# The last 1 MB of a batched 64x64 matmul: two stores of 512 KB by GpSimd in place of four of 256 KB by SyncE and ScalarE

## The chip, the core and the metric

The kernel runs on one core of a Trainium2 chip. The metric is the device time of one execution in microseconds (us). Three runs of the kernel before gave 128.67, 128.90 and 128.98 us, median 128.9 us. The profile comes from an execution of its own, told below.

## What is computed

```python
def reference(a, b):          # a, b: [1024, 64, 64] float32
    return np.matmul(a, b).astype(np.float32)
```

There are 1024 independent products of 64x64 matrices. Inputs are 2 x 16 MB, the output is 16 MB, all in float32.

## The kernel before, in words

**Tiling.** The output is worked off in `n_t` = 16 tiles of 64 matrices (1 MB each, `t` = 0 to 15); inputs are loaded for 128 matrices at a time (`s` = 0 to 7). For each tile, matrices of `a` are transposed (`turn_a`, VectorE), spread into a block-diagonal tile (`spread`, VectorE with some ScalarE), matrices of `b` are cast and turned (`turn`), and `products` (L201) multiplies four matrices at a time on TensorE into PSUM. `evacuate` (L238) copies the products from PSUM into the tile `o_sb`, which holds the whole result tile: 128 partitions x 8 groups (`gh`) x 1 KB. In the last tile (L269 to L273) the 16 steps go through four PSUM tiles of four steps each. ScalarE evacuates the first and third, VectorE the second and fourth, in four copies each (L247). So after ScalarE's first four copies groups 0 and 1 of `o_sb` are ready, after VectorE's first four groups 2 and 3, after ScalarE's last four groups 4 and 5, and after VectorE's last four groups 6 and 7.

**Stores.** `multiply` leaves a list of closures in `held[t]` (L280), which `store(t)` (L193) calls after the tile's work has been written down. Each closure calls `put(lo, n)` (L255), which starts one DMA from `n` groups of `o_sb` to `o_v[t]`. In HBM each partition's group is a run of 1 KB. For tiles 0 to 14, `put` writes four groups (512 KB) and `store_queue` (L80) names GpSimd. For the last tile, `put` writes two groups (256 KB), four times, and the queue comes from `LAST_QUEUE` (L51): SyncE for `lo` = 0, 2 and 6, ScalarE for `lo` = 4.

**Queues.** Nearly all loads, and the stores of tiles 0 to 14, are issued by GpSimd, on one queue that the profile names q0 (software_dynamic). SyncE's DMAs are on q1, ScalarE's on q10 (both hardware_dynamic). All of them are served by the core's 16 DMA engines. The order of the instructions on each engine is the order in the program text (`tc.manual_schedule`, L282). A store by GpSimd takes one of eight completion semaphores in turn and first waits until that semaphore's previous DMA has landed.

**The end.** After the last tile SyncE waits in turn for the semaphores of all DMAs and engines, every engine drains, and two rounds of barriers follow (L353 in the profile).

Of the kernel before, what the change touches and what calls it, by code (L numbers as in the profile page):

```python
# [12 lines left out]
def kernel(  # L13
# [14 lines left out]
    nc = tc.nc  # L28
# [4 lines left out]
    n_t, n_s = B // 64, B // 128  # L33
# [14 lines left out]
    }  # L48
    PAIRS = (1, 2, 3, 4, 5, 6, 7)
    BY_QUARTERS = (0, 1)  # L50
    LAST_QUEUE = {0: nc.sync, 2: nc.sync, 4: nc.scalar, 6: nc.sync}  # L51
    B_QUEUE = {0: nc.sync, 1: nc.scalar}

    a_v = a.rearrange("(s g h) (mp v) k -> s h g mp (v k)", h=4, g=32, v=16)
# [21 lines left out]
    warm = consts.tile([128, 2], fp32)  # L76
    a_tiles, b_tiles, at_tiles, bbf_tiles = {}, {}, {}, {}
    held = {}

    def store_queue(t, lo):  # L80
        return nc.gpsimd if t < n_t - 1 else LAST_QUEUE[lo]

    def load_a(s, hs=range(4)):
        if 0 in hs:
# [116 lines left out]
    def products(t, g0, n, o_ps, us=(0, 1)):  # L201
        bd = bd_tiles[t % N_BD]
        b_bf = bbf_tiles[t // 2][:, 16 * (t % 2) : 16 * (t % 2) + 16]
        split = len(us) == 1
        if t == n_t - 2:
            at_bd = bd[:].rearrange("p g w h mp vo -> p w g (h mp vo)")
            at_bd = at_bd.bitcast(bf16).rearrange("p w g (c u) -> p w g c u", u=2)
            steps = [
                (g, w, u, g % 2)
                for even in range(g0, g0 + n, 2)  # L210
                for w in range(4)
                for u in us
                for g in (even, even + 1)
            ]
        else:
            at_bd = bd[:].rearrange("p g (j wl) h mp vo -> p j g (wl h mp vo)", j=2)
            at_bd = at_bd.bitcast(bf16).rearrange("p j g (c u) -> p j g c u", u=2)
            steps = [(g, j, u, None) for g in range(g0, g0 + n) for j in range(2) for u in us]
        for g, w, u, par in steps:
            gl = (g - g0) // 2  # L220
            if par is None:
                place = o_ps[:, gl, 2 * (g % 2) + w, :]
                first = gl % 2 == 0 and w == 0 and g % 2 == 0
                final = gl % 2 == 1 and w == 1 and g % 2 == 1
            else:
                place = o_ps[64 * par : 64 * par + 64, gl, w, :]
                first = gl % 2 == 0 and w == 0
                final = gl % 2 == 1 and w == 3
            nc.tensor.matmul(  # L229
                place,  # L230
                at_bd[:, w, g, :, u],
                b_bf[:, g, 64 * u : 64 * u + 64],
                start=u == 0 and (first or not split),
                stop=u == 1 and (final or not split),
                skip_group_check=split,
            )

    def evacuate(t, g0, n, o_ps, o_sb, copy):  # L238
        rows = o_sb[:, g0 // 2 : (g0 + n) // 2]
        if t == n_t - 2:  # L240
            copy(rows, o_ps[:])
            return
        rows = rows.rearrange("p gh (j wl) n -> p gh j wl n", j=2)
        o_ps = o_ps[:].rearrange("p gl (par j) n -> p gl par j n", par=2)
        for par in range(2):
            for wl in range(2):
                copy(  # L247
                    rows[64 * par : 64 * par + 64, :, :, wl, :],
                    o_ps[64 * wl : 64 * wl + 64, :, par, :, :],
                )  # L250

    def multiply(t):
        o_sb = o_pool.tile([128, 8, 4, 64], fp32, name="o_sb")

        def put(lo, n):  # L255
            store_queue(t, lo).dma_start(  # L256
                out=o_v[t, :, lo : lo + n, :],
                in_=o_sb[:, lo : lo + n].rearrange("p gh w n -> p (gh w n)"),
            )

        act, dve = nc.scalar.copy, nc.vector.tensor_copy
        if t == n_t - 2:
            halves = [o_psum.tile([128, 4, 4, 64], fp32, name="o_ps") for _ in range(2)]
            for u in range(2):
                for half in range(2):
                    products(t, 8 * half, 8, halves[half], (u,))
                    if u == 1:
                        evacuate(t, 8 * half, 8, halves[half], o_sb, act)
        elif t == n_t - 1:  # L269
            for g0 in range(0, 16, 4):  # L270
                o_ps = t_psum.tile([128, 2, 4, 64], fp32, name="t_ps")
                products(t, g0, 4, o_ps)
                evacuate(t, g0, 4, o_ps, o_sb, dve if g0 % 8 else act)  # L273
        else:
            for g0 in (0, 8):
                o_ps = o_psum.tile([128, 4, 4, 64], fp32, name="o_ps")
                products(t, g0, 8, o_ps)
                evacuate(t, g0, 8, o_ps, o_sb, act)
        n = 2 if t == n_t - 1 else 4
        held[t] = [lambda lo=lo: put(lo, n) for lo in range(0, 8, n)]  # L280

    with tc.manual_schedule():  # L282
        load_first_a()
# [27 lines left out]
        for t in range(n_t):  # L311
            s, half = t // 2, t % 2
            multiply(t)
            if t == 1:
                spread_all(3)
            elif half == 0 and s + 1 < n_s and t:
                turn_a(s + 1, 0)
                turn_a(s + 1, 1)
                spread_all(t + 2)
            elif half and s + 1 < n_s:  # L320
                if s + 1 == n_s - 1:
                    spread_all(t + 2)
                turn(s + 1, 0)
                turn(s + 1, 1)
                if s + 1 < n_s - 1:
                    spread_all(t + 2)
            store(t)
# [30 lines left out]
```

## Time and profile before

| | us |
|---|---|
| median of 3 runs (lowest to highest) | 128.9 (128.67 to 128.98) |
| the profiled execution's own time | 128.72 |
| its span, first to last instruction | 126.9 |
| busy: DVE / ACT / POOL / PE | 104.0 / 93.7 / 64.1 / 53.1 |
| bytes: HBM read / written | 33.55 MB / 16.78 MB |
| share of the 16 DMA engines' span: q0 / q1 / q10 | 87.8% / 6.6% / 4.9% |

The span is shorter than the execution's own time by 1.8 us, which lie before the first and after the last instruction. The profile's rows give, for each line of the kernel, the engine, the operation, its output and input tiles, and busy time with the mean of one. POOL is GpSimd, SP is SyncE, and a "q" behind an engine's name stands for its sequencer, which issues DMAs and waits. Clock times are us from the start of the span. A DMA issue is the instruction that starts a transfer. Its landing is when the last of the 16 DMA engines has reported; each engine reports for itself, and these landing events are in the trace.

### The profile page before, as it was taken

The page shows a single profiled execution, that of the slowest core. Times are in us where ns is not written, and L with a number is a line of the kernel's source. Part 1 is how long each engine was busy: PE and PEld are TensorE (multiplying, and loading weights), DVE is VectorE, ACT ScalarE, POOL GpSimd, SP SyncE. Part 2 cuts the span into 40 slices and gives each one's busy share as a digit, 9 for nine tenths or more (in the row PEclk, how much of TensorE's full clock was granted, in tenths as well). Part 3 has the DMA queues.
Part 4 walks back from the last instruction along what each step waited for, and adds up shares of the span by engine and source line. Part 5 has one row for each costly group of instructions (what it writes and reads, how often), then busy time and mean ns, then how long its engine had stood idle before and what let it go on. Part 6 is the DMA issues. An engine that isn't in the chain of part 4 may idle for free.

```text
span 126.9 us, 2686 instructions
## 1 busy us (share of the span) xinstructions
PE 53.1 (42%) x1088; PEld 50.1 (39%) x1088; DVE 104.0 (82%) x109; ACT 93.7 (74%) x146; POOL 64.1 (50%) x92
## 2 busy tenths in 40 slices
PE   0000005740945057825751677057810863079200
PEld 0000005730935057815750677057800853079100
DVE  4998993499999999999999997995949789780900
ACT  2258019999396969997999799959897299999700
POOL 8981217973546545545574545475555564333100
PEclk9999999999595555555775555955555579756995
DMA  2999999999999999999999999999999999999993
GB/s 62 379 368 307 305 285 212 219 212 209 288 283 254 275 294 297 285 285 267 271 274 303 297 287 275 263 271 283 305 288 289 270 275 275 383 401 396 345 342 104
DMA packets 10123, 35.81 MB, mean 282 GB/s; under 512 B 1536, under 2 KB 2560, under 8 KB 8448
## 3 DMA queue, kind: packets, MB, share of 16 engines
q0 software_dynamic: 7392, 30.41, 87.8%
q1 hardware_dynamic: 1632, 2.88, 6.6%
q10 hardware_dynamic: 1088, 2.36, 4.9%
q8 instruction: 8, 0.13, 0.4%
q14 instruction: 3, 0.02, 0.0%
HBM read 33.55 MB, written 16.78 MB: 396 GB/s over the span
## 4 chain that ended last, share of the span: by engine, by line
DMA 62%; POOL 9%; ACT 8%; DVE 6%; issue 6%; PE 4%; DVEq 0%; POOLq 0%
DMA b_sb<-in_b_dram 32%; DMA a_sb<-in_a_dram 15%; DMA out_dram<-o_sb 15%; ACT o_sb L247 6%; DVE b_bf L127 4%; PE o_ps L229 3%; POOL at_bd L289 3%; POOL at_bd L302 3%; DVE o_sb L247 2%; POOL a_sb L89 2%; ACT at_bd L173 2%; PE t_ps L229 1%; POOL out_dram L256 1%; POOL b_sb L119 0%; DVEq L353 0%
## 5 line engine op out<-in xcount | busy, mean ns | idle before, releaser
L229 PE MATMUL o_ps<-b_bf,at_bd 128*128 128x64 bf16 (+1 forms) x1024 | 50.8, 230 | 65.0 <-ACT o_sb L247 25.9
L229 PEld LDWEIGHTS <-at_bd 128*128 128x128 bf16 (+1 forms) x1088 | 50.1, 125 | 67.9 <-issue 42.5
L247 ACT COPY o_sb<-o_ps 64x512 f32<-64x512 f32 x112 | 64.9, 580 | 11.2 <-PE o_ps L229 9.7
L256 POOL DMA_DIRECT2D out_dram<-o_sb x30 | 24.4, 814 | 28.3 <-ACT o_sb L247 9.3
L127 DVE STREAM_TRANSPOSE b_bf<-b_sb 128x1024 f32<-128x1024 f32 x14 | 29.8, 2182 | 3.3 <-DMA b_sb<-in_b_dram 3.2
L150 DVE STREAM_TRANSPOSE at_sb<-a_sb 128x1024 f32<-128x1024 f32 x12 | 22.5, 1947 | 2.7 <-issue 1.3
L173 DVE COPY at_bd<-at_sb 32x1024 f32<-32x1024 f32 x34 | 23.8, 700 | 1.0
L92 POOL DMA_DIRECT2D a_sb<-in_a_dram x24 | 14.0, 585 | 18.3 <-DMA a_sb<-in_a_dram 10.5
L119 POOL DMA_DIRECT2D b_sb<-in_b_dram x28 | 15.9, 576 | 6.8 <-DMA out_dram<-o_sb 5.6
L163 DVE COPY at_bd<-at_sb 32x512 f32<-32x512 f32 x30 | 13.1, 438 | 3.8 <-POOL at_bd L302 3.2
L173 ACT COPY at_bd<-at_sb 32x1024 f32<-32x1024 f32 x14 | 14.6, 1043 | 2.0 <-DVE at_sb L150 1.8
L191 ACT CAST b_bf<-b_sb 128x2048 bf16<-128x2048 f32 x2 | 3.7, 1896 | 6.1 <-DMA b_sb<-in_b_dram 6.1
L247 DVE COPY o_sb<-t_ps 64x256 f32<-64x256 f32 x8 | 3.4, 422 | 3.5 <-PE t_ps L229 3.4
L135 ACT CAST a_bf<-o_sb 128x1024 bf16<-128x1024 f32 x3 | 3.0, 1044 | 4.0 <-DMA o_sb<-in_a_dram 4.0
L140 DVE STREAM_TRANSPOSE at_sb<-a_bf 128x512 f32<-128x512 f32 x4 | 4.1, 1050 | 0.4 <-ACT a_bf L135 0.3
L140 DVE STREAM_TRANSPOSE at_sb<-a_sb 128x512 f32<-128x512 f32 x4 | 3.9, 1034 | 0.4 <-DMA a_sb<-in_a_dram 0.4
L288 DVE MEMSET at_bd<- 128x4096 f32 x1 | 3.5, 3472 | 0.8 <-issue 0.8
L289 POOL MEMSET at_bd<- 128x4096 f32 x1 | 3.5, 3511 | 0.3 <-POOLq L342 0.3
L302 POOL MEMSET at_bd<- 128x4096 f32 x1 | 3.5, 3530 | 0.0
L285 ACT ACT_TABLE_LOAD x1 | 1.3, 1283 | 2.3 <-issue 2.3
L247 ACT COPY o_sb<-t_ps 64x256 f32<-64x256 f32 x8 | 2.9, 367 | 0.1
L89 POOL DMA_DIRECT2D a_sb<-in_a_dram x4 | 2.7, 692 | 0.0
(11 smaller groups left out, 7.2 us busy)
## 6 DMA issues: line engine op xcount, KB each, us to landing
out_dram<-o_sb POOLq DMA_DIRECT2D x30, 512.0 KB, 9.4
a_sb<-in_a_dram POOLq DMA_DIRECT2D x28, 256.0 KB, 9.6
b_sb<-in_b_dram POOLq DMA_DIRECT2D x28, 256.0 KB, 9.6
o_sb<-in_a_dram ACTq DMA_DIRECT2D x2, 512.0 KB, 6.8
o_sb<-in_a_dram SPq DMA_DIRECT2D x2, 512.0 KB, 5.8
out_dram<-o_sb SPq DMA_DIRECT2D x3, 256.0 KB, 5.2
out_dram<-o_sb ACTq DMA_DIRECT2D x1, 256.0 KB, 5.1
b_sb<-in_b_dram SPq DMA_DIRECT2D x1, 0.5 KB, 15.9
```

The costliest lines, as they stand in the source:

```text
L92: nc.gpsimd.dma_start(out=rows, in_=ap_v[s, h])
L119: nc.gpsimd.dma_start(out=pair[32 * h : 32 * h + 32, 0], in_=bp_v[s, h])
L127: nc.vector.transpose(cols[:, u], rows[:, u])
L140: nc.vector.transpose(at_tiles[s][:, h].rearrange("p g w mp vo -> p w vo g mp"), rows.bitcast(fp32).rearrange("p (vo w kp) -> p w vo kp", ...
L150: nc.vector.transpose(cols[:, 2 * h : 2 * h + 2].rearrange("p mp vo w g -> p (mp vo) w g"), rows[:, 2 * h : 2 * h + 2].rearrange("p mp vo ...
L163: copy(bd[rows, 8 * i : 8 * i + 8, :, h, :, :].rearrange("p g w mp vo -> p (g w) (mp vo)"), at_sb[block : block + 32, h].rearrange("p g w ...
L173: copy(bd[rows, :, :, h, :, :].rearrange("p g w mp vo -> p (g w) (mp vo)"), at_sb[rows, half].rearrange("p g w mp vo -> p (g w) (mp vo)"),)
L229: nc.tensor.matmul(place, at_bd[:, w, g, :, u], b_bf[:, g, 64 * u : 64 * u + 64], start=u == 0 and (first or not split), stop=u == 1 and ( ...
L247: copy(rows[64 * par : 64 * par + 64, :, :, wl, :], o_ps[64 * wl : 64 * wl + 64, :, par, :, :],)
L256: store_queue(t, lo).dma_start(out=o_v[t, :, lo : lo + n, :], in_=o_sb[:, lo : lo + n].rearrange("p gh w n -> p (gh w n)"),)
L289: nc.gpsimd.memset(bd_tiles[1][:], 0.0)
L302: nc.gpsimd.memset(bd_tiles[2][:], 0.0)
```

## The change

The last tile is stored as all the others are: by GpSimd, in two DMAs of four groups (512 KB). The two quarters of a half that were separate DMAs are now one, so it waits for both ScalarE's and VectorE's copies of that half. `LAST_QUEUE` and `store_queue` go.

```diff
-    LAST_QUEUE = {0: nc.sync, 2: nc.sync, 4: nc.scalar, 6: nc.sync}
...
-    def store_queue(t, lo):
-        return nc.gpsimd if t < n_t - 1 else LAST_QUEUE[lo]
...
         def put(lo, n):
-            store_queue(t, lo).dma_start(
+            nc.gpsimd.dma_start(
                 out=o_v[t, :, lo : lo + n, :],
                 in_=o_sb[:, lo : lo + n].rearrange("p gh w n -> p (gh w n)"),
             )
...
-        n = 2 if t == n_t - 1 else 4
-        held[t] = [lambda lo=lo: put(lo, n) for lo in range(0, 8, n)]
+        held[t] = [lambda lo=lo: put(lo, 4) for lo in (0, 4)]
```

## The prediction

> **What bounds the kernel now.** The change touches only the last tile's stores, so I read the end of the kernel and leave the rest. First the time by stage (sums of PE, PEld, DVE, ACT and POOL, then the granted clock, the busy share of the DMA engines and GB/s):
>
> ```profile
> 113.00:115.00 2.00, 1.92 (x73) 1.79 (x70) 0.83 (x1) 1.81 (x3) 0.73 (x1) 0.50 1.01 397
> 115.00:117.00 2.00, 2.00 (x62) 1.94 (x58) 0.00 (x0) 2.00 (x3) 0.72 (x1) 0.62 1.03 393
> 117.00:119.00 2.00, 1.11 (x39) 0.99 (x34) 1.72 (x5) 1.93 (x6) 0.79 (x2) 1.00 1.02 352
> 119.00:121.00 2.00, 0.00 (x0) 0.00 (x0) 1.66 (x4) 0.80 (x3) 0.00 (x0) 1.00 0.97 345
> 121.00:123.00 2.00, 0.00 (x0) 0.00 (x0) 0.00 (x0) 0.00 (x0) 0.00 (x0) 1.00 1.01 341
> 123.00:125.00 2.00, 0.00 (x0) 0.00 (x0) 0.00 (x0) 0.00 (x0) 0.00 (x0) 0.59 0.87 294
> ```
>
> From 121 on no engine computes any more, and the DMA engines are still full: the end is set by the backlog of stores. The second thing to see is the last column. The same full engines move 393 to 397 GB/s up to 117 and 341 to 352 GB/s after it, although until 119.8 only GpSimd's queue has data packets. So the pace of a store at the very end is not the pace of a store before.
>
> Second, the timeline of the end (start, length):
>
> ```profile
> 114.98 1.93 ACT L241 COPY o_sb<-o_ps 128x1024 f32<-128x1024 f32 x2 [0.16 <-PE o_ps L229]
> ...
> 116.79 3.03 ACT L247 COPY o_sb<-t_ps 64x256 f32<-64x256 f32 x8
> 117.20 0.75 POOL L256 DMA_DIRECT2D out_dram<-o_sb  x1 [0.16 <-issue]
> 117.22 3.49 DVE L247 COPY o_sb<-t_ps 64x256 f32<-64x256 f32 x8 [3.39 <-PE t_ps L229]
> 118.32 2.81 SPq L256 DMA_DIRECT2D out_dram<-o_sb  x3
> 119.85 0.40 ACTq L256 DMA_DIRECT2D out_dram<-o_sb  x1
> ```
>
> The data of the last tile are complete at 117.22 + 3.49 = 120.71, and the last quarter is issued at 120.73 (SyncE's third). Third, the time from issue to landing, over all stores:
>
> ```profile
> out_dram<-o_sb POOLq DMA_DIRECT2D x30, 512.0 KB, 9.4
> ...
> out_dram<-o_sb SPq DMA_DIRECT2D x3, 256.0 KB, 5.2
> out_dram<-o_sb ACTq DMA_DIRECT2D x1, 256.0 KB, 5.1
> ```
>
> The landing events give the order. GpSimd's last eight stores have their last engine's report at 113.24, 114.54, 115.85, 117.13, 118.42, 119.74, 121.35 and 123.34. The steps are 1.30, 1.31, 1.28, 1.29, 1.32, then 1.61 and 1.99. The four quarters land at 123.54, 124.25, 124.98 and 125.66. The last one opens the close: SyncE goes through its remaining waits at 0.06 us each, is drained at 126.18, and two rounds of barriers end at 126.9, which is 1.24 us behind the last landing. Fourth, GpSimd has a drain of its own in the close:
>
> ```profile
> L353 POOLq DRAIN  x1: 6697/6697/6697, 117.2 to 117.2; - x1
> ```
>
> It ends at 117.18 + 6.70 = 123.88, which is 0.53 us behind the last landing of GpSimd's own queue (123.34). Now it ends 2.3 us ahead of SyncE and costs nothing.
>
> **The change part by part.**
>
> *Removed: four issues and their waits.* SyncE's three (0.40, 0.84 and 0.41 us) and ScalarE's one (0.40 us) lie behind no compute of theirs and beside a full DMA backlog. ScalarE has no work after 119.82. Worth nothing by themselves. Their transfers go too: 1024 packets of 1 KB at a mean of 48.2 ns, over 16 engines 3.08 us.
>
> *Added: two issues by GpSimd.* GpSimd issues 0.29 us after its producer ends (ScalarE's L241 pair ends at 116.91, the issue starts at 117.20), where SyncE needs 0.03 us, and an issue takes it 0.75 us. The first half waits for VectorE's fourth copy, 118.94: issue at 119.23 to 119.98. The second waits for VectorE's eighth, 120.70: issue at 120.99 to 121.74. Nothing is queued on GpSimd behind them but its drain. The semaphores whose turn it is were last used by the stores that landed at 113.24 and 114.54, so no wait for a semaphore is added. The first quarter was issued at 118.32 and could move from then on; now nothing of the last tile moves before 119.23. That 0.9 us is covered while GpSimd's queue is not empty: alone, its packets in flight at 119.78 are still 1.87 us of work for each engine, so they end near 121.65 on average.
>
> Is the cover enough? A GpSimd store in a short queue is the one issued at 116.28: its first engine reported 3.58 us after the issue, the last 5.06 us after. By this the first half is down between 122.81 and 124.29, the second between 124.57 and 126.05. The 5.06 holds some waiting behind the store ahead, so this is no firm floor, but it leaves little to spare: if the cover is gone, the second half lands up to 126.05.
>
> The Trainium skill (DMA: Bandwidth & Descriptors, section "Latency and other measured facts") gives about 0.6 us to the first byte for a DMA of SyncE or ScalarE and about 1 us for one of GpSimd, which speaks against the change: by it the two halves would cost 0.4 us where the queue is empty and nothing where it is not. No run here shows a first byte with an empty queue.
>
> *Moved: 1 MB from q1 and q10 to q0.* The two halves are 256 packets of 4 KB. Their duration is what I can't read off for sure. By the packets of 113 to 115 it is 165 ns; in 120 to 122 it is 187 ns. For the engine that is last, the step from one store's last landing to the next shows the same: 1.30 us in the steady part, 1.61 us for the store of 116.28, when only one or two stores stood ahead of it and no other queue moved much. The third, 1.99, shared its engines with the quarters, so it is left out. From 121.35, when the store of 116.28 is down, three stores remain (that of 117.20, now alone, and the two halves):
>
> - at 1.30 each: 121.35 + 3.90 = 125.25, against 125.66 before: 0.41 us earlier;
> - at 1.61 each: 121.35 + 4.83 = 126.18: 0.52 us later.
>
> I take 1.61. At the end never more than two stores wait, as with the row that gave 1.61; the 1.30 comes from rows with four and more in flight. Both ends are kept for the range.
>
> *The close.* SyncE's waits behind the last landing are about as many as now (two HWDGE semaphores fewer in the list, GpSimd's ones nearer to its start): 0 to 0.1 us. What is late next is GpSimd's drain. Now it must outlast the last landing of the kernel: if it ends 0.53 us behind it, as before, that is 126.18 + 0.53 = 126.71, and SyncE is through at 126.18 + 0.52 = 126.70. They tie: nothing added.
>
> **Sum.** +0.52 on the end, 0 in the close: span 126.9 + 0.5 = 127.4, and 128.72 + 0.52 = 129.24 for the profiled execution. The median of the runs is 0.18 above the profiled execution's time, so the forecast for the runs is 128.9 + 0.5 = **129.4 us**.
>
> **The rivals.** A measurement of this kernel can tell about 0.3% (0.39 us) from no change; so "same" is 128.5 to 129.3.
>
> 1. *GpSimd's queue keeps its steady pace* (faster). The 4 KB packets take 165 ns, the two halves need 2 x 8 x 0.165 = 2.64 us on each engine where the quarters need 3.08 us: 0.44 less by packets, 0.41 less by the steps: 128.5 us. For it: 165 ns stays the 25th percentile of GpSimd's packets right to 121. Against it: the rate fell to 345 GB/s with that queue alone. It decides if the step is at or under 1.30.
>
> 2. *Bytes are bytes* (same). From 117 on the engines move 341 to 352 GB/s whether the packets are GpSimd's or the quarters'. If that rate is the limit, 1 MB takes as long through either queue and the end stays: a step near 1.45 gives 121.35 + 4.35 = 125.70, +0.04 us: 128.9 us. For it: the flat last column. Against it: the slowest engine, not the mean, ends the kernel, and on GpSimd's queue its report came up to 1.1 us behind the mean one (store of 117.20), on the last quarter 0.6 us behind. The Trainium skill (same page, section "Issuing engines are not separate DMA queues") states this rival: the DMAs of all issuers run on the same 16 engines, and another issuer saves only issue time. By it the sum would be zero.
>
> 3. *The drain becomes the bound* (slower still). If GpSimd's drain is not tied to the landing but takes a fixed time after its last issue (123.88 - 117.95 = 5.92 us), it now ends at 121.74 + 5.92 = 127.66. The barrier that began at 126.20 then begins at 127.68: +1.48 us, 130.4 us. For it: one profile can't tell the two apart. Against it: an end 0.53 us behind the last landing looks like a wait for the transfers.
>
> **How the numbers follow.** Forecast (+0.5, slow step) 0.42; rival 1 0.20; rival 2 0.28; rival 3 0.10. Slower is the forecast and rival 3, 0.52; same 0.28; faster 0.20. The range goes from rival 1 (128.5) to rival 3 (130.4); the forecast with its neighbours alone would be 129.0 to 129.8.
>
> **What would show it.** GpSimd's last two issues at 119.2 and 121.0, each 0.75 us. The steps between the last landings of GpSimd's last three stores: 1.6 means the forecast, 1.45 rival 2, 1.3 rival 1. The rate in 121 to 125. The end of GpSimd's drain: 0.5 us behind the last landing is the forecast's, and near 127.7 with landings by 126.2 is rival 3. I am wrong if a first packet of the second half comes after the queue ran dry for long (a gap in the DMA share near 122.5 to 123.5), or if the stores of tile 14 themselves land at other times.

## The result and the profile after

The changed kernel takes 128.94 us (median of 14 runs, 128.76 to 129.11), the kernel before, beside it, 128.73 us (14 runs, 128.55 to 129.02). The ratio is 1.0016 with a 95% interval of 1.0009 to 1.0024: **0.21 us slower** (0.12 to 0.31). The interval leaves no doubt that it is slower, but the loss is less than half of the forecast 0.5 us, and 128.94 lies inside what the prediction called "same". The profiled execution of the changed kernel has its own time of 128.95 us and a span of 127.2 us.

The timeline of the end, in the changed kernel (start, length; lines are four or five lower than before):

```profile
116.67 3.02 ACT L243 COPY o_sb<-t_ps 64x256 f32<-64x256 f32 x8
117.07 0.75 POOL L252 DMA_DIRECT2D out_dram<-o_sb  x1 [0.16 <-issue]
117.17 3.48 DVE L243 COPY o_sb<-t_ps 64x256 f32<-64x256 f32 x8 [3.47 <-PE t_ps L225]
119.44 0.75 POOL L252 DMA_DIRECT2D out_dram<-o_sb  x1 [1.61 <-DVE o_sb L243]
121.20 0.75 POOL L252 DMA_DIRECT2D out_dram<-o_sb  x1 [1.01 <-issue]
```

What starts between 116 and 117.2 does so 0.05 to 0.13 us earlier than before. GpSimd's two new issues come at 119.44 and 121.20, each 0.55 us behind VectorE's copy (118.89 and 120.65). The stages of the end, with the columns as before:

```profile
113.00:115.00 2.00, 1.92 (x72) 1.78 (x70) 0.70 (x1) 1.81 (x3) 0.60 (x1) 0.50 1.02 399
115.00:117.00 2.00, 2.00 (x59) 1.94 (x56) 0.00 (x0) 2.00 (x3) 0.75 (x1) 0.61 1.02 385
117.00:119.00 2.00, 1.06 (x37) 0.94 (x33) 1.76 (x5) 1.92 (x7) 0.75 (x1) 1.00 1.00 348
119.00:121.00 2.00, 0.00 (x0) 0.00 (x0) 1.61 (x4) 0.69 (x2) 0.75 (x1) 0.74 1.02 360
121.00:123.00 2.00, 0.00 (x0) 0.00 (x0) 0.00 (x0) 0.00 (x0) 0.75 (x1) 0.50 0.93 315
123.00:125.00 2.00, 0.00 (x0) 0.00 (x0) 0.00 (x0) 0.00 (x0) 0.00 (x0) 0.50 0.83 293
```

The DMA engines are no longer quite full in 121 to 123 (0.93 against 1.01 before), so the queue did run partly dry. Yet the last landing moves little: 125.76 against 125.66. The landing events of GpSimd's last four stores are at 121.24, 122.81, 124.37 and 125.76, steps of 1.57, 1.56 and 1.39 us. The first two of these are the stores of tile 14, which landed at 121.35 and 123.34 before.

The rest of the loss is behind the last landing. These are the close's rows (L353 before, L348 after): count, shortest/median/longest in ns, and the starts of the first and the last. Before, from 125.6 on:

```profile
L353 SPq EVENT_SEMAPHORE  x7: 27/28/28, 125.7 to 126.0; - x7
L353 SPq DRAIN  x2: 7/10/13, 126.1 to 126.2; - x2
L353 POOLq EVENT_SEMAPHORE  x2: 17/17/17, 126.2 to 126.3; - x2
```

After, from 125.7 on:

```profile
L348 SPq EVENT_SEMAPHORE  x7: 28/28/28, 125.8 to 126.1; - x7
L348 SPq DRAIN  x2: 7/10/13, 126.2 to 126.3; - x2
L348 POOLq DRAIN  x1: 5202/5202/5202, 121.2 to 121.2; - x1
L348 POOLq EVENT_SEMAPHORE  x1: 17/17/17, 126.4 to 126.4; - x1
```

SyncE goes through seven waits in both, the first of which is the one for the last landing. It is drained at 126.18 before and at 126.28 after, 0.52 us behind the landing each time. But GpSimd's drain, over at 123.88 before, now ends at 121.18 + 5.20 = 126.38, which is 0.10 us after SyncE, and GpSimd's barrier wait (the last row) follows it. From the last landing to the end of the span it takes 1.40 us; before it took 1.28 (the prediction has 1.24, from a span rounded down to 126.9).

### The profile page after: what moved, and what is told of

Its sections match the earlier page's. It is cut to its first block, busy times and chain, and to the rows that moved or that the text cites. A ratio compares the mean times of both kernels' runs of the same rounds, so it can differ in the third digit from the quotient of the medians.

```text
span 127.2 us, 2684 instructions
## 1 busy us (share of the span) xinstructions
PE 54.3 (43%) x1088; PEld 51.3 (40%) x1088; DVE 103.9 (82%) x109; ACT 93.7 (74%) x146; POOL 64.8 (51%) x94
## 4 chain that ended last, share of the span: by engine, by line
DMA 48%; DVE 20%; POOL 10%; ACT 6%; issue 6%; PE 4%; POOLq 1%; DVEq 1%; ACTq 0%
DMA b_sb<-in_b_dram 26%; DMA a_sb<-in_a_dram 15%; DVE b_bf L123 9%; DMA out_dram<-o_sb 7%; ACT o_sb L243 5%; DVE at_bd L159 5%; DVE at_sb L146 3%; PE o_ps L225 3%; POOL at_bd L284 3%; POOL at_bd L297 3%; POOL a_sb L85 2%; DVE o_sb L243 2%; POOL out_dram L252 2%; PE t_ps L225 1%; DVE at_bd L169 1%
## 5 line engine op out<-in xcount | busy, mean ns | idle before, releaser
L225 PE MATMUL o_ps<-b_bf,at_bd 128*128 128x64 bf16 (+1 forms) x1024 | 52.0, 233 | 63.7 <-ACT o_sb L243 24.8
L225 PEld LDWEIGHTS <-at_bd 128*128 128x128 bf16 (+1 forms) x1088 | 51.3, 127 | 66.7 <-issue 41.9
L252 POOL DMA_DIRECT2D out_dram<-o_sb x32 | 26.4, 824 | 31.2 <-DMA a_sb<-in_a_dram 9.3
L115 POOL DMA_DIRECT2D b_sb<-in_b_dram x28 | 15.1, 547 | 7.6 <-DMA out_dram<-o_sb 5.7
```

What stands on the lines that cost most here:

```text
L115: nc.gpsimd.dma_start(out=pair[32 * h : 32 * h + 32, 0], in_=bp_v[s, h])
L225: nc.tensor.matmul(place, at_bd[:, w, g, :, u], b_bf[:, g, 64 * u : 64 * u + 64], start=u == 0 and (first or not split), stop=u == 1 and ( ...
L252: nc.gpsimd.dma_start(out=o_v[t, :, lo : lo + n, :], in_=o_sb[:, lo : lo + n].rearrange("p gh w n -> p (gh w n)"),)
```

## The experiments

The table has, from each kernel's profile, the last landing, the times at which SyncE and GpSimd are through with their drains, and the time from the last landing to the end of the span ("close"); then the time against the kernel before on the same chip, with its interval.

| | last landing | SyncE | GpSimd | close | against before |
|---|---|---|---|---|---|
| before | 125.66 | 126.18 | 123.88 | 1.28 | |
| changed | 125.76 | 126.28 | 126.38 | 1.40 | +0.16% (+0.09 to +0.24) |
| e1 four quarters, GpSimd | 126.09 | 126.46 | 126.79 | 1.48 | +0.33% (+0.21 to +0.44) |
| e2 two halves, SyncE | 125.65 | 125.80 | 123.38 | 0.92 | **-0.28% (-0.41 to -0.16)** |
| e3 half GpSimd, half SyncE | 125.77 | 125.93 | 125.24 | 0.93 | -0.23% (-0.34 to -0.13) |
| e4 half SyncE, half GpSimd | 125.72 | 126.37 | 126.30 | 1.43 | +0.09% (-0.02 to +0.20) |
| e5 before, 6 spare loads | 125.87 | 126.02 | 123.68 | 0.92 | -0.10% (-0.19 to -0.01) |
| e6 before, 7 spare loads | 126.04 | 126.62 | 123.91 | 1.35 | +0.39% (+0.25 to +0.53) |
| e7 changed, no wait for data | 126.06 | 126.58 | 126.68 | 1.40 | +0.37% (+0.19 to +0.55) |
| e8 changed, long queue | 126.13 | 126.65 | 126.75 | 1.40 | +0.43% (+0.30 to +0.57) |
| e9 e8, idle engines | 126.41 | 126.93 | 127.03 | 1.41 | +0.49% (+0.23 to +0.75) |
| e10 changed, reversed places | 126.01 | 126.53 | 126.63 | 1.40 | +0.08% (-0.07 to +0.23) |

A landing differs by some 0.1 to 0.25 us between profiles of kernels whose stores are alike (changed and e10: 125.76 and 126.01). The close does not: 1.40 or 1.41 in all five kernels with two GpSimd stores at the end. In all twelve profiles, 0.77 to 0.79 us are left from the later of the two drains to the end of the span, so the close is that later drain and a fixed rest.

Landings can be compared more closely with two means over the 16 DMA engines' reports: that of the last store, less that of the store which GpSimd issues near 106 us in every kernel. This is 10.08 to 10.12 us in the four kernels whose last tile goes out by SyncE and ScalarE (before, e2, e5, e6), 10.24 and 10.27 with one half by GpSimd (e3, e4), 10.30 to 10.34 with all of it by GpSimd and issued when its data are ready (changed, e1, e10), and 10.24, 10.21 and 10.11 in e7, e8 and e9, where the stores don't wait for their data.

### e1 to e4: which engine issues what

My theories were a late start of GpSimd's stores (S), the pace of its packets (P) and its drain (D).

```diff
 e1  LAST_QUEUE = {0: nc.gpsimd, 2: nc.gpsimd, 4: nc.gpsimd, 6: nc.gpsimd}
 e2  LAST_QUEUE = {0: nc.sync, 4: nc.sync}      # with n = 4
 e3  LAST_QUEUE = {0: nc.gpsimd, 4: nc.sync}    # with n = 4
 e4  LAST_QUEUE = {0: nc.sync, 4: nc.gpsimd}    # with n = 4
```

(All four are edits of the kernel before.)

> The last tile goes out in four stores of 256 KB, all by GpSimd. Theory S (late start: an issue by GpSimd that waits for two engines starts 0.55 us after the later one and takes 0.75 us, so the queue runs partly dry in 121 to 123, DMA share 0.92): a quarter can start before its half is complete, the first near 118.7 instead of 119.4, and the queue is fuller; the last landing is some 0.2 us earlier than with halves, the time within 0.1 us of before. Theory D (GpSimd's drain is the last thing, about 0.1 us later than SyncE's waits): its drain still ends last, 0.6 us behind the last landing. Theory P (the pace of GpSimd's packets, 187 ns for 4 KB at the end, sets it): no gain from quarters, as late as with halves, +0.2 us.

**e1** came out at 129.21 against 128.77 us, more than any of the theories had. S is wrong here: the first quarter was issued at 118.37, a microsecond earlier than the first half in the changed kernel (119.44), the DMA share stayed at 1.00 to 1.02 up to 123, and the last landing was later, not earlier. The packets in 121 to 123 took 202 to 204 ns on average; with halves they took 190 to 194. D is right, and seen better than in the changed kernel, since the semaphore of the last quarter is later in SyncE's list, with four waits behind it:

```profile
L353 SPq EVENT_SEMAPHORE  x5: 28/28/1194, 124.9 to 126.3; - x5
L353 SPq DRAIN  x2: 7/10/13, 126.4 to 126.5; - x2
L353 POOLq DRAIN  x1: 6340/6340/6340, 120.4 to 120.4; - x1
L353 POOLq EVENT_SEMAPHORE  x1: 17/17/17, 126.8 to 126.8; - x1
```

SyncE is drained at 126.46, but the barrier waits for GpSimd's drain until 120.45 + 6.34 = 126.79, 0.70 us behind the last landing.

> The last tile goes out in two stores of 512 KB, both by SyncE. S: SyncE issues 0.03 us behind the producer, at 118.97 and 120.73, so the backlog covers the start and the time is that of before within 0.1 us. If it is the size (halves against quarters) that costs, it is as late as the change, +0.2 us. D: GpSimd's drain ends near 123.9 as before and costs nothing. P: packets of 1 KB at 48 ns as before, so 3.1 us for 1 MB, no change.

**e2** is faster than both kernels: 128.37 against 128.77 us. No theory of mine had that. The last landing is that of before to 0.01 us. The close is 0.92 in place of 1.28 us, 0.36 less, and the runs gained 0.40. The rows of the close show why (from 125.6 on):

```profile
L353 SPq DRAIN  x2: 7/10/13, 125.7 to 125.8; - x2
L353 SPq EVENT_SEMAPHORE  x1: 27/27/27, 125.7 to 125.7; - x1
L353 POOLq EVENT_SEMAPHORE  x1: 17/17/17, 125.8 to 125.8; - x1
```

One wait is left behind the landing, where before there were seven. Transfers by SyncE and ScalarE take eight completion semaphores in turn. Six go to the loads at the start, so the two halves take the seventh and eighth, which SyncE waits for last. With quarters, the third and fourth come round to the first and second semaphore, which stand early in SyncE's list; when the last quarter lands, the rest of the list is still to be gone through, at 0.06 us each.

The DMA rate is near that of GpSimd's queue, although two thirds of the bytes in the window below are moved in SyncE's packets of 1 KB:

```profile
121.00:123.00 2.00, 0.00 (x0) 0.00 (x0) 0.00 (x0) 0.00 (x0) 0.00 (x0) 0.85 1.01 340
```

> First half by GpSimd, second half by SyncE, 512 KB each. D: GpSimd's drain follows the landing of the first half (near 124.4) and ends near 125, ahead of SyncE's waits; the 0.1 us of the drain is gone. S: only the first half starts late (119.4), the second is issued at 120.7; the gap near 121 to 122 stays, the one near 122 to 123 goes: +0.05 to +0.1 us over before. P: half of the loss of the change, +0.1 us.

> First half by SyncE, second half by GpSimd, 512 KB each. D: GpSimd's drain ends 0.6 us behind the last landing, so the 0.1 us stays. S: the first half is issued at 118.97 and fills the gap that the first half by GpSimd left; the second is issued by GpSimd near 121.2 and should come while the first is still moving: landings as before, the time +0.1 us by the drain alone. P: +0.1 us.

**e3 and e4** send the same two halves through the same two queues, in opposite order. The landings differ by 0.05 us, the closes by 0.50 (0.93 and 1.43), and the times by 0.42 us (128.51 and 128.93). So the close tells them apart. First e3, from 125.7 on (the second of the two waits belongs to the barrier), then e4:

```profile
L353 SPq EVENT_SEMAPHORE  x2: 17/22/28, 125.8 to 126.1; - x2
...
L353 SPq EVENT_SEMAPHORE  x9: 28/28/28, 125.7 to 126.2; - x9
L353 POOLq DRAIN  x1: 4891/4891/4891, 121.4 to 121.4; - x1
```

In e3 GpSimd's drain ends 0.58 us behind its own half, ahead of SyncE, and SyncE has one wait left. In e4 SyncE has nine waits left, the one for the last landing among them, and GpSimd's drain is through 0.07 us before SyncE: both are late at once, as in the changed kernel. The gain of e3 doesn't refute the +0.1 us that P and S gave: its close is 0.36 us shorter than before, and its last landing is 0.11 us later.

### e5 and e6: another turn of the semaphores

```diff
+    spare = consts.tile([128, 8, 16], fp32)
+    rows = a[0:2].rearrange("b m k -> (b m) k")
...
+            if t == 3:
+                for i in range(6):        # 7 in e6
+                    nc.sync.dma_start(out=spare[:, i], in_=rows[:, 0:16])
             multiply(t)
```

> The kernel before (quarters by SyncE and ScalarE), with six spare loads of 8 KB issued by SyncE in the middle of the kernel, whose data nobody uses. They take six turns of the eight completion semaphores of SyncE and ScalarE, so that the last quarter gets the semaphore that SyncE waits for last at the close. Theory C (the close: how many waits of 0.06 us SyncE has still to go through after the last landing sets the time, not the landing): last landing as before, the time from it to the end 0.92 us in place of 1.28, so 0.36 us faster than before, 128.4 us. Theory Q (SyncE's halves were faster for their size or their fewer issues): no change, or slower by what the spare loads cost, 128.7 to 128.9 us.

> The same with seven spare loads, so that the last quarter gets a semaphore that SyncE waits for early in the close. C: seven or eight waits of 0.06 us follow the last landing, 1.28 to 1.40 us from it to the end, so 0 to 0.1 us slower than before and 0.4 us slower than with six spare loads, 128.8 us. Q: the same as with six spare loads.

The stores are those of before, quarter by quarter; e6 is e5 with one spare load more. In e5, from 125.8 on:

```profile
L358 SPq DRAIN  x2: 7/10/13, 126.0 to 126.0; - x2
L358 SPq EVENT_SEMAPHORE  x1: 28/28/28, 125.9 to 125.9; - x1
L358 POOLq EVENT_SEMAPHORE  x1: 17/17/17, 126.0 to 126.0; - x1
```

In e6, from 126.0 on:

```profile
L358 SPq EVENT_SEMAPHORE  x8: 28/28/28, 126.1 to 126.5; - x8
L358 SPq DRAIN  x2: 7/10/13, 126.6 to 126.6; - x2
L358 POOLq EVENT_SEMAPHORE  x1: 17/17/17, 126.6 to 126.6; - x1
```

One spare load of 8 KB more, issued more than 100 us before the end, gives eight waits behind the landing in place of one, and a close of 1.35 in place of 0.92 us. The runs differ by 0.59 us (128.75 and 129.34). Of that, 0.43 is the close, and 0.17 lies in the landings of these two profiles, which the theory doesn't explain. Against the kernel before, both missed what was expected: e5 gained 0.19 us where 0.36 was expected, and e6 lost 0.40 where at most 0.1 was. Their last landings are 0.21 and 0.38 us later than before, as their stores were from 109 on (the store of 109.33 before is issued at 109.76 in e5 and at 109.99 in e6). The spare loads weren't free: no data hold SyncE back in the loop, so they were issued not in the middle but from 3.3 us on, among the first loads. Theory C, the close, holds, by the rows and by e5 against e6. Theory Q would have e5 and e6 alike, and they aren't; e5's time alone would have fitted Q.

### e7 to e10: what sets the pace of the landings

```diff
 e7  results[t] = o_sb is kept for each tile; the stores of t = 15 read results[t - 1], the result tile of t = 14
 e8  the stores of t = 14 and 15 read results[t - 2]
 e9  e8, and for t >= 14 no products(...) and no evacuate(...)
 e10 out=o_v[n_t - 1 - t, ...]      # changed kernel otherwise
```

> The changed kernel, but the two stores of the last tile read the result tile before it, so the last tile's result isn't written and its stores wait for no copy of the last tile; they are issued by 119. Theory S (a late start leaves the queue partly dry): DMA share back to 1.0 in 121 to 124 (0.95 in the changed kernel), last landing 0.2 to 0.3 us earlier than there. Theory P (the pace of packets at the end, 185 to 190 ns, is there whatever stands ahead): the steps between last landings stay near 1.5 us, no more than 0.1 us earlier. If more stores ahead bring the pace back to 165 ns, the steps shrink towards 1.3 us and it lands 0.5 us earlier.

**e7** does not show the gain that S expected: with both halves issued by 118.66 + 0.75 = 119.41 the DMA share was 1.00 to 1.02 up to 123, and the last landing was 126.06, no earlier than with the gaps.

```profile
119.00:121.00 2.00, 0.00 (x0) 0.00 (x0) 1.46 (x4) 0.76 (x3) 0.41 (x1) 1.00 1.00 330
121.00:123.00 2.00, 0.00 (x0) 0.00 (x0) 0.00 (x0) 0.00 (x0) 0.00 (x0) 0.99 1.02 346
```

A full queue did not help; the packets took longer (206 and 197 ns on average in 120 to 121 and 121 to 122, against 188 and 190 in the changed kernel). By the means above, e7 is 0.06 to 0.10 us better than the changed kernel and e10, so that much of S may be there.

> As the run before, but the stores of the last two tiles read the two tiles before them (the last two results aren't written), so six stores or more stand in GpSimd's queue from 114 on. If the short queue makes packets slow: 165 ns and 400 GB/s to the end, steps of 1.30 us, last landing near 124.9, 0.8 us earlier than in the changed kernel. If it is something else at that time (the place in HBM, the copies of ScalarE and VectorE): packets of 185 ns from 117 on all the same, last landing near 125.5.

**e8** refutes my reading that a short queue makes the packets slow. Its five stores were issued back to back from 113.11 on:

```profile
113.00:115.00 2.00, 1.90 (x70) 1.77 (x69) 0.98 (x1) 1.92 (x2) 1.89 (x3) 0.50 1.03 406
115.00:117.00 2.00, 2.00 (x61) 1.94 (x58) 0.00 (x0) 1.86 (x3) 1.83 (x3) 0.57 1.01 358
117.00:119.00 2.00, 1.28 (x44) 1.16 (x40) 1.57 (x4) 1.94 (x7) 0.00 (x0) 1.00 1.03 344
119.00:121.00 2.00, 0.00 (x0) 0.00 (x0) 1.80 (x5) 0.95 (x3) 0.00 (x0) 1.00 1.00 352
```

With five stores waiting, the rate still falls from 406 to 344 GB/s, and the fall comes a microsecond or two earlier than in the changed kernel (358 against 385 in 115 to 117). The last landing, 126.13, is later than either expectation had it.

> As e8 (the stores of the last two tiles read the two tiles before them, whose copies are long done), and the products of the last two tiles and their copies out of PSUM are left out too, so TensorE, VectorE and ScalarE have little or nothing to do from 114 on. If the copies or the products slow the DMA engines' packets at the end: 165 ns and 390 to 400 GB/s to the end, steps of 1.30 us, last landing 0.7 us earlier than in e8. If they don't: packets of 185 to 190 ns in the last 7 us all the same, last landing within 0.2 us of e8.

> The changed kernel with the result tiles written in reversed places: tile t goes to the place of tile 15 - t, so the last stores write the first MB of the output. If the place in HBM makes the last packets slow: the last stores keep 165 ns and 1.30 us a step, last landing 0.5 us earlier than in the changed kernel. If not: the same 185 to 190 ns from 117 on, the time as the changed kernel, +0.2 us over before.

In **e9** TensorE, VectorE and ScalarE have nothing to do from 115 on; the rate is 350, 350 and 346 GB/s from 117 to 123 all the same:

```profile
117.00:119.00 2.00, 0.00 (x0) 0.00 (x0) 0.00 (x0) 0.00 (x0) 0.00 (x0) 0.50 1.01 350
```

**e10** writes the last tiles to the other end of the output; 348 GB/s in 117 to 119 and steps of 1.55, 1.65 and 1.38 us. So the slower pace is not made by the late start, a short queue, the copies and products, or the place in HBM. In every run it begins some six to eight microseconds after the last load has landed (109.1 to 110.0), when only stores are left; whether that is its cause was not tried, and in e8 and e9, whose stores are issued earlier, it begins sooner than in the others. **What makes it stays open.** What the runs do show is that the rate is about the same for both queues: 340 GB/s in e2 and 346 in e7, in 121 to 123.

e7, e8 and e9 issue their stores earlier than the changed kernel and yet took longer (+0.37% to +0.49% against +0.16%), with the same close. What grew is the distance between the DMA engines: from the first engine's report of the last store to the last one's it is 1.01 us in the changed kernel, 1.50 in e7, 1.95 in e8 and 2.49 in e9. The mean of the 16 reports stays near: 125.15, 125.30, 125.24 and 125.10. Why the engines drift apart was not tried.

## Why the prediction was wrong

The sign was right, in part by luck: over half of the loss, 0.12 of 0.21 us, is in the close, which the sum put at nothing, and the rest, 0.09 us (0.00 to 0.19 by the interval), is in the landing, which the sum put at 0.52. Of its steps:

- **The step that failed: "at 1.61 each ... I take 1.61".** The three steps came to 1.57, 1.56 and 1.39, 4.52 us together, not 4.83. The row with 1.61 was a single step between single engines' reports, in one profile; the mean landing of that same store is 1.52 behind the one before it, and in the changed kernel 1.50. With +0.10 us at the last landing instead of +0.52, this term was mis-sized by 0.42: 0.31 by the steps, and 0.11 because the store from which they are counted landed at 121.24, not 121.35 (other times of tile 14's stores were among the prediction's signs of being wrong). The reason given, a short queue that makes GpSimd's packets slow, was wrong too: with a full queue the steps stay near 1.5 (e7, e8), and SyncE's stores meet the same rate (e2). The profile before could have told: the store of 112.97 had five stores ahead of it, and its mean landing already came 1.51 us behind the one before it, while its last engine's report came 1.32 behind. And the store of 116.28 had three ahead when it was issued, not "one or two".
- **"They tie: nothing added" in the close** was wrong by 0.12 us. The tie between SyncE and GpSimd's drain was seen rightly and lost narrowly: the drain ended 0.62 us behind the landing, not 0.53, and later than SyncE by 0.10. The larger oversight is that the close was taken as fixed. It can be had at 0.92 us (e2, e3, e5), and the 0.36 us between that and the kernel before is more than the whole change.
- **The 0.29 us from the producer's end to GpSimd's issue** were 0.55. GpSimd's issue has two engines and its semaphore to wait for, and the wait for VectorE, which ends last, stands in a separate instruction ahead of it; the row was from a store with a single wait. It moved both issues by 0.2 us; by e7 an earlier issue doesn't bring the last landing forward.
- **"The cover is enough, with little to spare"**: it wasn't quite (share 0.93 in 121 to 123), and the runs show little that it cost: e7, with no gap, is 0.06 to 0.10 us better by the means and has no earlier last landing. The Trainium skill's first bytes (DMA: Bandwidth & Descriptors, "Latency and other measured facts"), from which the prediction worked out 0.4 us, can't be tried here either: no run shows a first byte with an empty queue.
- **Rival 2, bytes are bytes, was nearly right on the landings.** The mean landing of the last store is 125.05 before, 125.15 after, 124.95 in e2 and 125.30 in e7, whoever issues. This is what the Trainium skill says on the same page ("Issuing engines are not separate DMA queues"), and these numbers agree to 0.35 us. Counted from the store of 106, there is a difference left: a last tile all by GpSimd lands 0.18 to 0.26 us later than one by SyncE and ScalarE (in e7 to e9 at most 0.16); what makes it isn't shown. Rival 2's change was +0.04 us, and that its 128.9 us came out is luck: the kernel before had its median at 128.73 beside the changed one, not at 128.9. What it lacked is that the issuer also decides the close.
- **Rival 1** (steady pace) did not occur in any run. **Rival 3** (a drain of fixed length) is refuted by the profile: 126.38 - 121.95 = 4.43 us behind the last issue, not 5.92, and in all runs 0.53 to 0.70 us behind GpSimd's last landing. That the drain becomes the bound was right, at less than a tenth of the price (0.10 us behind SyncE, not 1.48).

The range held the time; the size of the change, +0.21 us for +0.5, was missed.

## What to carry to other kernels

When the end of a kernel is a backlog of stores, moving a store to another issuing engine may move its landing little (here by 0.26 us at most); look also at what follows the last landing. Count the waits that SyncE still has to go through (0.06 us each here), and see whose drain ends last: letting the last transfer take a semaphore that is waited for at the end of the list, and keeping GpSimd out of the last store, was worth 0.36 us of 128.7, for an edit of two lines (e2, two halves by SyncE: the runs were 0.28% faster than before). And a step between single last landings is too coarse for a forecast of some tenths of a microsecond; the mean over the 16 engines, counted from an earlier store, repeats better (10.08 to 10.12 us in four kernels, where the last engine's reports give 9.54 to 9.81).

## What was unexpected of the hardware

- GpSimd's drain ends 0.53 to 0.70 us behind its last landing in all twelve profiles, and the barriers wait for it.
- With only stores left, the full DMA engines fall from about 400 to about 345 GB/s; 4 KB packets go from 165 ns to between 185 and 200 ns, and 1 KB packets of SyncE's queue take 48 ns, which is the same rate (4 x 48 = 192 ns for 4 KB).
- A full queue did not beat a queue with gaps: in 119 to 123 the changed kernel moved 360 and 315 GB/s at shares of 1.02 and 0.93, e7 330 and 346 at 1.00 and 1.02, the same bytes in all.
